# Dividing the attention probabilities by their sums: by a diagonal of reciprocals inside the turning product, in place of a multiplication on GpSimd

## The chip, the core and the metric

The kernel runs on one core of a Trainium2 chip. The metric is the device time of one execution in microseconds (us). A core has five engines that each work through a queue of their own in order: TensorE (PE in the profile, its weight loads PEld), VectorE (DVE), ScalarE (ACT), GpSimd (POOL) and SyncE (SP, which here issues most transfers). They wait for one another by semaphores.

## The reference

One layer: a normalised and modulated input is projected once; half of the width goes through an RWKV-7 recurrence, half through latent attention with 8 heads of 64 (scores over 64 + 32 rotary columns); both halves are gated, projected back and normalised. What the change touches is the attention of 1024 queries over 1024 keys:

```python
def causal_block_attention(q_nope, q_rope, k_nope, k_rope, v):
    scale = (MLA_NOPE + MLA_ROPE) ** -0.5
    ...
    s = (jnp.einsum('bqhd,bkhd->bhqk', qn_b, k_nope)
         + jnp.einsum('bqhd,bkd->bhqk', qr_b, k_rope)).astype(jnp.float32) * scale
    s = jnp.where(key_idx[None, :] <= q_idx[:, None], s, -jnp.inf)
    prob = jax.nn.softmax(s, axis=-1).astype(v.dtype)
    return jnp.einsum('bhqk,bkhd->bqhd', prob, v)
```

So each row of probabilities is the exponential of the scores less their maximum, divided by its own sum.

## The kernel before

Products that need more precision than one pass of TensorE gives are made of three: each operand is split into a high and a low part (type fp32r), and high by high, high by low and low by high are added in PSUM. The program has three long stretches. Up to about 650 us of the span the projections, the recurrence and the preparation of queries, keys and values run interleaved. From 650 to about 822 us the attention runs. From there to the end the output projection (lines 1160 to 1162) and the last normalisation run.

The attention is a loop over 64 steps (`seq`, lines 1196 to 1240): four pairs of heads, in each pair two heads, in each head eight blocks i = 0 to 7 of 128 queries. A step with block i handles (i + 1) blocks of 128 keys, since the rest is masked; a head thus has 1 + 2 + ... + 8 = 36 blocks of 128 x 128, and the stage 288. The parts of a step are:

- `scores` (lines 1059 to 1074): three products per half of the keys into `sp` (PSUM, two buffers), and a small one in bf16 that adds the causal mask.
- `softmax_a` (line 1079): the row maximum `mx` on VectorE, scaled on line 1080.
- `softmax_b`: the exponential on ScalarE from `sp` to `pr` (SBUF, three buffers), which also gives the row sums `sm` (line 1087); the reciprocal on VectorE (line 1088); and the multiplication of `pr` by it on GpSimd, in pieces of up to 512 columns (line 1091).
- `turn_pe` (line 1098): for each block of 128 keys a transpose of `pr` on TensorE into `tp` (PSUM, two buffers of four blocks), so that keys lie on the partitions.
- `turn_evac`: the high part `PTh` on ScalarE (line 1107), the low part `PTl` on VectorE (line 1108).
- `mix` (lines 1119 and 1120): once for two blocks of queries, the values times `PTh` and `PTl` into `op` (PSUM); `gate` (lines 1134 and 1136): two copies on ScalarE (`oc`, `od`), two operations on GpSimd.

In loop step t the program writes the scores and the maximum of step t + 2, the turning of step t, the mixing of steps before, and then the exponential, the reciprocal and the division of step t + 2. So between the end of a division and its turning two steps lie. The queries and keys of the next pair (`heads_qk`, lines 828 to 830, with copies on lines 847 and 848) and the weights for them are spread over the same steps. A scheduler of the framework sets the final order of each engine's queue from this text and its own costs; the loop asks for a priority that keeps near the written order.

Of the kernel before, what the change touches and what calls it, by code (L numbers as in the profile page):

```python
# [17 lines left out]
F32 = mybir.dt.float32  # L18
# [4 lines left out]
ALU = mybir.AluOpType  # L23
# [4 lines left out]
P = 128  # L28
# [3 lines left out]
HALF = 512  # L32
# [54 lines left out]
def hymba_kernel(ctx: ExitStack, tc: tile.TileContext, x, pos, cols, cst, winit, w_ada, b_gate, w_in, w_lora, w0,  # L87
                 w_uqn, w_uqr, w_k, w_v, w_out, final_g, out, dbg=None):
    nc = tc.nc
    V, A, G, T, SY = nc.vector, nc.scalar, nc.gpsimd, nc.tensor, nc.sync  # L90
# [5 lines left out]
    def pool(stack, name, bufs=1, **kw):  # L96
        if kw.get("space") is not DRAM:
            kw["reuse_waits"] = "tile"
        return stack.enter_context(tc.tile_pool(name=name, bufs=bufs, **kw))
# [12 lines left out]
    def cs(name):  # L112
        a, n = _CS[name]
        return cstt[:, a: a + n]

    ident = cs("ident")
# [52 lines left out]
    evp = pool(ctx, "evp")  # L169
# [885 lines left out]
    V.tensor_scalar(rsn[:], rs[0][:], -SCALE, None, ALU.mult)  # L1055

    PTs, probs, tail, ocs, od = {}, {}, [], {}, {}

    def scores(hp, s, i):

# [22 lines left out]
    def softmax_b(i, sp, mx):  # L1083
        n = (i + 1) * P
        pr = at.tile([P, S], F32, tag="pr", name="pr", bufs=3)
        sm = at.tile([P, 1], F32, tag="sm", name="sm", bufs=4)
        A.activation(pr[:, 0:n], sp[:, 0:n], AF.Exp, scale=rss[:, i:i + 1], bias=mx[:], accum_out=sm[:])  # L1087
        V.reciprocal(sm[:], sm[:])  # L1088
        for a in range(0, n, HALF):
            e = min(n, a + HALF)  # L1090
            G.tensor_scalar(pr[:, a:e], pr[:, a:e], sm[:], 1.0, ALU.mult, ALU.mult)  # L1091
        return pr

    def turn_pe(hp, s, i, j0, pr):
        m = min(4, i + 1 - j0)
        tp = psB.tile([P, 4, P], F32, tag="tp", name="tp", bufs=2)
        for j in range(m):
            T.transpose(tp[:, j, :], pr[:, (j0 + j) * P:(j0 + j + 1) * P], ident)  # L1098
        return tp

    def turn_evac(hp, s, i, j0, tp):
# [93 lines left out]
    with tc.high_priority(offset=0):  # L1195
        for t in range(-AHEAD, N + 2):
            sp = mx = op = None
            if 0 <= t + AHEAD < N:
                hp, s, i = seq[t + AHEAD]
# [8 lines left out]
            if sp is not None:  # L1208
                hp, s, i = seq[t + AHEAD]
                mx = softmax_a(i, sp)  # L1210
            if 0 <= t < N:
                hp, s, i = seq[t]
# [6 lines left out]
            if t >= 2 and seq[t - 2][2] % 2 == 1:  # L1219
                hp, s, i = seq[t - 2]  # L1220
                op = mix(hp, s, i // 2)
            if sp is not None:
                probs[t + AHEAD] = softmax_b(seq[t + AHEAD][2], sp, mx)
            if op is not None:
                hp, s, i = seq[t - 2]
# [160 lines left out]
```

## Time and profile before

| | us |
|---|---|
| median of 3 runs | 933.34 |
| the runs | 2558.89, 925.86, 933.34 |
| the profiled execution, its own time | 920.99 |
| its span, first to last instruction | 918.8 |
| granted TensorE clock, mean over the span | 0.973 |

| stretch of the span, us | length | PE | DVE | ACT | POOL busy |
|---|---|---|---|---|---|
| 0 to 650 | 650 | 590.32 | 396.49 | 310.56 | 182.05 |
| 650 to 822 (attention) | 172 | 156.11 | 134.94 | 139.27 | 87.05 |
| 822 to 918.8 | 96.8 | 88.89 | 43.85 | 26.64 | 27.08 |

A line of the profile names the line of the kernel, the engine, the operation, the tile that is written and the ones that are read, and how often it ran. Matmuls follow each other in a pipeline: a record's duration goes on after the next one has started, so what a matmul costs in a row of them is the distance between two starts, not its duration. Of the runs, 2558.89 us is not used.

### The profile page before, as it was taken

How to read it: one execution, taken by the hardware profiler on the slowest of the kernel's cores; microseconds unless marked ns; L12 is line 12 of the kernel's file. 1: busy time of each engine (PE TensorE's matmuls, PEld its weight loads, DVE VectorE, ACT ScalarE, POOL GpSimd, SP SyncE). 2: the span in 40 equal slices, each digit the busy share in tenths (PEclk: the TensorE clock that was granted, in tenths of full speed). 3: DMA queues.
4: the chain of work that ended last, by engine and by line, in shares of the span. 5: the costliest groups of instructions: out<-in, count | busy, mean ns of one | idle time of the engine just before them, and what ended most of it. 6: DMA issues, size and time to landing. Idle time of an engine off the chain costs nothing.

```text
span 918.8 us, 16567 instructions
## 1 busy us (share of the span) xinstructions
PE 835.3 (91%) x5812; PEld 641.2 (70%) x5812; DVE 575.3 (63%) x1462; ACT 476.5 (52%) x1112; POOL 296.2 (32%) x351
## 2 busy tenths in 40 slices
PE   1798997999999999898899999997799998989996
PEld 0586785776777777566667767765678777868885
DVE  5795349378495654955757366247778788765443
ACT  2655332444644636346245464554778888873311
POOL 1311423131232323423133122223436454454400
PEclk9999999999999999998999999999999999999998
DMA  8764433333435324435333254157102031017233
GB/s 253 247 194 153 140 110 115 95 105 88 134 118 150 118 69 135 121 69 165 118 99 104 65 151 139 49 172 203 55 18 70 21 110 59 1 56 239 85 126 126
DMA packets 131714, 106.66 MB, mean 116 GB/s; under 512 B 40616, under 2 KB 108464, under 8 KB 131632
## 3 DMA queue, kind: packets, MB, share of 16 engines
q1 hardware_dynamic: 130672, 102.46, 37.5%
q0 software_dynamic: 960, 3.15, 1.5%
q8 instruction: 46, 0.75, 0.3%
q14 instruction: 36, 0.29, 0.1%
HBM read 76.46 MB, written 29.10 MB: 115 GB/s over the span
## 4 chain that ended last, share of the span: by engine, by line
PE 66%; DVE 13%; ACT 9%; issue 4%; DMA 4%; POOL 2%; SPq 1%; POOLq 0%; DVEq 0%; ACTq 0%
PE mm L164 10%; PE mm L165 8%; PE mm L166 8%; PE po L1160 3%; PE po L1162 3%; PE po L1161 3%; PE gps L577 3%; ACT pr L1087 2%; DVE wtmp L625 2%; DVE W L627 2%; PE tp L1098 2%; ACT PTh L1107 1%; PE rc L712 1%; PE rc L694 1%; PE Y L728 1%
## 5 line engine op out<-in xcount | busy, mean ns | idle before, releaser
L164 PE MATMUL mm<-hTh,whi 128*128 128x512 f32 (+1 forms) x384 | 167.2, 435 | 3.1 <-DVE wtmp L625 2.3
L166 PE MATMUL mm<-hTh,wlo 128*128 128x512 f32 (+1 forms) x384 | 156.9, 409 | 0.0
L165 PE MATMUL mm<-hTl,whi 128*128 128x512 f32 (+1 forms) x384 | 156.8, 408 | 0.0
L157 POOL TENSOR_TENSOR wlo<-wraw,whi 128x512 fp32r<-128x512 f32 (+1 forms) x54 | 71.4, 1323 | 233.8 <-ACT whi L156 215.4
L164 PEld LDWEIGHTS mm<-hTh,whi 128*128 128x128 f32 (+1 forms) x384 | 73.3, 191 | 24.0 <-issue 3.1
L166 PEld LDWEIGHTS mm<-hTh,wlo 128*128 128x128 f32 (+1 forms) x384 | 73.2, 191 | 17.7
L165 PEld LDWEIGHTS mm<-hTl,whi 128*128 128x128 f32 (+1 forms) x384 | 73.5, 191 | 14.6 <-issue 1.4
L1091 POOL TENSOR_SCALAR pr<-pr,sm 128x512 f32<-128x512 f32 (+2 forms) x96 | 55.6, 588 | 72.4 <-DVE sm L1088 50.2
L627 DVE TENSOR_TENSOR W<-W,wtmp 128x60 f32<-128x60 f32 (+24 forms) x248 | 71.5, 288 | 5.8 <-DVE wtmp L625 0.3
L625 DVE TENSOR_TENSOR wtmp<-W,N 128x60 f32<-128x60 f32 (+24 forms) x248 | 69.2, 279 | 5.5
L156 ACT CAST whi<-wraw 128x512 fp32r<-128x512 f32 (+1 forms) x54 | 32.7, 607 | 59.4 <-PE mm L165 36.6
L720 ACT ACTIVATE ST<-rc,eL 64x64 f32<-64x64 f32 x120 | 37.1, 309 | 46.2 <-PE rc L712 44.5
L1087 ACT ACTIVATE pr<-sp,mx,rss 128x128 f32<-128x128 f32 (+3 forms) x64 | 53.3, 834 | 14.8 <-DVE mx L1080 12.3
L1108 DVE TENSOR_TENSOR PTl<-tp,PTh 128x512 fp32r<-128x512 f32 (+2 forms) x96 | 52.2, 553 | 11.8 <-ACT PTh L1107 10.1
L1079 DVE TENSOR_REDUCE mx<-sp 128x1 f32<-128x128 f32 (+3 forms) x64 | 48.0, 750 | 11.4 <-PE sp L1073 11.1
L1160 PE MATMUL po<-wo,yh 128*128 128x512 f32 x128 | 50.3, 393 | 0.8 <-ACT od L1134 0.8
L1107 ACT CAST PTh<-tp 128x512 fp32r<-128x512 f32 (+2 forms) x96 | 44.0, 477 | 13.1 <-PE tp L1098 10.2
L1098 PE MATMUL tp<-cstt,pr 128*128 128x128 f32 x288 | 45.0, 277 | 5.9 <-POOL pr L1091 2.9
L1162 PE MATMUL po<-wo,yl 128*128 128x512 f32 x128 | 50.3, 393 | 0.0
L1161 PE MATMUL po<-wo,yh 128*128 128x512 f32 x128 | 50.3, 393 | 0.0
L1119 PE MATMUL op<-PTh,Vt 128*128 128x256 f32 (+1 forms) x160 | 42.1, 293 | 5.1 <-ACT od L1134 5.1
L584 DVE TENSOR_TENSOR GA<-gps,cstt 128x512 f32<-128x512 f32 x32 | 21.4, 684 | 29.4 <-PE Y L728 22.6
(279 smaller groups left out, 1934.0 us busy)
## 6 DMA issues: line engine op xcount, KB each, us to landing
wraw<-in_w_in SPq DMA_DIRECT2D x52, 256.0 KB, 3.1
wa<-in_w_ada SPq DMA_DIRECT2D x64, 128.0 KB, 3.1
xt<-in_x SPq DMA_DIRECT2D x8, 512.0 KB, 7.4
wg<-in_w_ada SPq DMA_DIRECT2D x32, 128.0 KB, 2.5
N<-d_n SPq DMA_DIRECT2D x32, 128.0 KB, 3.1
wor<-in_w_out SPq DMA_DIRECT2D x16, 256.0 KB, 3.1
cr<-d_c SPq DMA_DIRECT2D x14, 256.0 KB, 3.4
d_c<-craw SPq DMA_DIRECT2D x10, 256.0 KB, 2.2
```

What stands on the lines that cost most here:

```text
L157: G.tensor_tensor(lo[:, :, :m], raw[:, :, :m], hi[:, :, :m].bitcast(F32), ALU.subtract)
L164: T.matmul(ps[:m], lhsT=hi[:, k % 4, :m], rhs=a, start=first, stop=False)
L165: T.matmul(ps[:m], lhsT=hi[:, k % 4, :m], rhs=b, start=False, stop=False)
L166: T.matmul(ps[:m], lhsT=lo[:, k % 4, :m], rhs=a, start=False, stop=last)
L625: V.tensor_tensor(t, W[:, 0:n, u:u + 1].to_broadcast([P, n, m]), N[:, u:u + 1, u + 1:32].to_broadcast([P, n, m]), ALU.mult)
L627: V.tensor_tensor(W[:, 0:n, u + 1:32], W[:, 0:n, u + 1:32], t, ALU.subtract)
L1087: A.activation(pr[:, 0:n], sp[:, 0:n], AF.Exp, scale=rss[:, i:i + 1], bias=mx[:], accum_out=sm[:])
L1091: G.tensor_scalar(pr[:, a:e], pr[:, a:e], sm[:], 1.0, ALU.mult, ALU.mult)
L1098: T.transpose(tp[:, j, :], pr[:, (j0 + j) * P:(j0 + j + 1) * P], ident)
L1160: T.matmul(ps, lhsT=yh[k][:, ts_], rhs=hi, start=first, stop=False)
L1161: T.matmul(ps, lhsT=yh[k][:, ts_], rhs=lo, start=False, stop=False)
L1162: T.matmul(ps, lhsT=yl[k][:, ts_], rhs=hi, start=False, stop=last)
```

## The change

The multiplication of the whole of `pr` by the reciprocals goes. In its place GpSimd multiplies the 128 x 128 identity by the reciprocals of the step's 128 rows, which gives a diagonal matrix `dg`, one of four in a new tile `dgs`. The turning is no longer a transpose with the identity but a plain FP32 product of the block of `pr` (stationary) with `dg` (moving): a transpose whose columns are divided by the sums. `dgs` takes one of the two buffers of the tag `p2`, which is shared with the normalisation of the recurrence (`post`) and with the squares of the last stage (line 1286 before).

```diff
@@ -1055,6 +1055,7 @@
     PTs, probs, tail, ocs, od = {}, {}, [], {}, {}
+    dgs = evp.tile([P, 4, P], F32, tag="p2", name="dgs", bufs=2)
 
@@ -1086,16 +1087,17 @@
         V.reciprocal(sm[:], sm[:])
-        for a in range(0, n, HALF):
-            e = min(n, a + HALF)
-            G.tensor_scalar(pr[:, a:e], pr[:, a:e], sm[:], 1.0, ALU.mult, ALU.mult)
-        return pr
-
-    def turn_pe(hp, s, i, j0, pr):
+
+        dg = dgs[:, i % 4]
+        G.tensor_scalar(dg, ident, sm[:], 1.0, ALU.mult, ALU.mult)
+        return pr, dg
+
+    def turn_pe(hp, s, i, j0, prob):
+        pr, dg = prob
         m = min(4, i + 1 - j0)
         tp = psB.tile([P, 4, P], F32, tag="tp", name="tp", bufs=2)
         for j in range(m):
-            T.transpose(tp[:, j, :], pr[:, (j0 + j) * P:(j0 + j + 1) * P], ident)
+            T.matmul(tp[:, j, :], lhsT=pr[:, (j0 + j) * P:(j0 + j + 1) * P], rhs=dg, start=True, stop=True)
         return tp
```

The scheduler also orders the queues a little differently in the attention; outside it the order stays. Lines behind line 1058 move down by one, behind line 1091 by two. Three places show it.

GpSimd, in the third pair of heads (`wor` and `gb` belong to the output projection, `yg` and `oc` to `gate`). Before:

```order
L1153 TENSOR_TENSOR wor<-wor,gb 128x512
L1091 TENSOR_SCALAR pr<-pr,sm 128x256
L1136 TENSOR_TENSOR oc<-oc,od 128x256
L1136 TENSOR_TENSOR yg_7452<-oc,yg_7452 128x256
L1091 TENSOR_SCALAR pr<-pr,sm 128x384
L1091 TENSOR_SCALAR pr<-pr,sm 128x512
```

With the change:

```order
L1155 TENSOR_TENSOR wor<-wor,gb 128x512
L1092 TENSOR_SCALAR dgs<-cstt,sm 128x128 x2
L1138 TENSOR_TENSOR oc<-oc,od 128x256
L1138 TENSOR_TENSOR yg_7445<-oc,yg_7445 128x256
L1092 TENSOR_SCALAR dgs<-cstt,sm 128x128 x2
```

One or two multiplications for a step, of up to 512 columns each, have become one of 128 columns for each of the 64 steps, and the diagonal of one step more stands ahead of the two operations of `gate`.

TensorE, in the second pair of heads, the turning of the step with block i = 5 (six blocks of keys) amid the mixing of the steps before. Before:

```order
L1119 MATMUL op<-PTh,Vt 128x256
L1120 MATMUL op<-PTl,Vt 128x256
L1098 MATMUL tp<-cstt,pr 128x128 x4
L1119 MATMUL op<-PTh,Vt 128x128
L1120 MATMUL op<-PTl,Vt 128x128
L1098 MATMUL tp<-cstt,pr 128x128 x2
L1069 MATMUL sp<-kt_6872,qt_6873 128x128
```

With the change:

```order
L1121 MATMUL op<-PTh,Vt 128x256
L1122 MATMUL op<-PTl,Vt 128x256
L1121 MATMUL op<-PTh,Vt 128x128
L1100 MATMUL tp<-dgs,pr 128x128 x6
L1122 MATMUL op<-PTl,Vt 128x128
L1070 MATMUL sp<-kt_6872,qt_6873 128x128
```

The six turnings now stand together, behind the last but one product of the mixing and ahead of the next scores.

ScalarE, a little further in the same pair. Before:

```order
L1087 ACTIVATE pr,sm<-sp,mx,rss 128x896
L1107 CAST PTh<-tp 128x4x128
L1134 COPY oc<-op 64x256
L1107 CAST PTh<-tp 128x2x128
L1134 COPY od<-op 64x256
L1087 ACTIVATE pr,sm<-sp,mx,rss 128x1024
```

With the change:

```order
L1088 ACTIVATE pr,sm<-sp,mx,rss 128x896
L1109 CAST PTh<-tp 128x4x128
L1109 CAST PTh<-tp 128x2x128
L1088 ACTIVATE pr,sm<-sp,mx,rss 128x1024
L1136 COPY oc<-op 64x256
L1136 COPY od<-op 64x256
```

The exponential of the widest block now stands ahead of the two copies that free `op`.

## The prediction

> **What bounds the kernel now.** I read the page from the top, then the busy time in the three stretches of the span, then the attention alone: its groups, its waits, and its instructions in order of time.
>
> ```profile
> span 918.8 us, 16567 instructions
> ```
>
> ```profile
> core 0: us, PE busy (x) PEld busy (x) DVE busy (x) ACT busy (x) POOL busy (x), PEclk, DMA share, GB/s
> 0.00:650.00 650.00, 590.32 (x4389) 437.58 (x4389) 396.49 (x1068) 310.56 (x724) 182.05 (x181) 0.97 0.45 131
> 650.00:822.00 172.00, 156.11 (x1039) 131.61 (x1039) 134.94 (x329) 139.27 (x330) 87.05 (x145) 1.00 0.15 46
> ```
>
> The change touches only the stretch from 650 to 822 us, the attention. There TensorE shows 156.11 us of 172 at full granted clock, so 15.9 us of open idle time; ScalarE 139.27, VectorE 134.94, GpSimd 87.05. What the change takes from, GpSimd, is the emptiest of the four, and what it adds to, TensorE, the fullest. What is removed and what waits on it, from the groups and the waits of that stretch:
>
> ```profile
> L1091 POOL TENSOR_SCALAR pr<-pr,sm 128x512 f32<-128x512 f32 (+2 forms) x96 | 55.6, 588 | 72.4 <-DVE sm L1088 50.2 <-DVE mx L1080 9.2 <-PE qkps L830 5.8
> ```
>
> ```profile
> PEld tp L1098 <- POOL pr L1091: 6.0, 10, 1.4
> ...
> PE tp L1098 <- POOL pr L1091: 2.9, 4, 1.1
> ```
>
> GpSimd multiplies for 55.6 us but stands idle 72.4 us before it, waiting for the sums: it follows the softmax, it does not hold it up much. TensorE waits for its result 14 times, 6.0 us seen from the weight loads and 2.9 from the matmuls. So the division is mostly latency that two steps of lead cover.
>
> How full TensorE really is, the busy time does not tell, because a record goes on after the next has started. The distances do:
>
> ```profile
> 699.61 0.39 PE L1069 MATMUL sp<-kt,qt 96*128 96x512 f32 x1
> 699.84 0.39 PE L1070 MATMUL sp<-kt,qt 96*128 96x512 f32 x1
> ...
> 700.29 0.28 PE L1069 MATMUL sp<-kt,qt 96*128 96x256 f32 x1
> 700.40 0.28 PE L1070 MATMUL sp<-kt,qt 96*128 96x256 f32 x1
> ...
> 701.39 0.22 PE L1119 MATMUL op<-PTh,Vt 128*128 128x128 f32 x1
> 701.45 0.27 PE L1120 MATMUL op<-PTl,Vt 128*128 128x128 f32 x1
> ...
> 702.91 0.34 PE L1070 MATMUL sp<-kt,qt 96*128 96x384 f32 x1
> 703.08 0.34 PE L1071 MATMUL sp<-kt,qt 96*128 96x384 f32 x1
> ```
>
> A matmul of 512 columns is followed after 0.23 us, of 384 after 0.17, of 256 after 0.11 to 0.12, of 128 after 0.06. The counts in the stretch, of which lines 1070, 1071 and 829, 830 repeat those of 1069 and 828, and 1120 that of 1119:
>
> ```profile
> L1098 PE MATMUL tp<-cstt,pr 128*128 128x128 f32 x288 | 45.0, 277 | 5.9 <-POOL pr L1091 2.9 <-DVE PTl L1108 2.6
> L1119 PE MATMUL op<-PTh,Vt 128*128 128x256 f32 x128 | 36.0, 309 | 5.1 <-ACT od L1134 5.1
> ...
> L1069 PE MATMUL sp<-kt,qt 96*128 96x512 f32 x48 | 20.8, 432 | 2.9 <-ACT pr L1087 2.9
> ...
> L828 PE MATMUL qkps<-cqh,wqh 128*128 128x512 f32 x18 | 8.3, 463 | 1.8 <-DVE mx L1080 1.2 <-DVE kt L848 0.6
> ...
> L1069 PE MATMUL sp<-kt,qt 96*128 96x384 f32 x16 | 5.9, 370 | 0.2 <-ACT pr L1087 0.2
> ...
> L828 PE MATMUL qkps<-ckvh,wkh 128*128 128x512 f32 x11 | 5.0, 459 | 0.0
> ...
> L1069 PE MATMUL sp<-kt,qt 96*128 96x256 f32 x15 | 4.4, 292 | 0.0
> ```
>
> Of 512 columns 3 x (48 + 18 + 11) = 231, 53 us; of 384, 3 x 16 = 48, 8 us; of 256, 2 x 128 + 3 x 15 = 301, 35 us; of 128 without the turning some 170, 11 us; the 288 transposes at 0.11 us, 31 us. Together 138 of 172 us: TensorE is the fullest engine, with 34 us in which nothing starts, of which 15.9 are open idle.
>
> **The change part by part.** *The turning.* It is the only price. A transpose and a plain FP32 product of the same size stand both in the trace of before, at full clock: line 536 (transposes) and line 524 (FP32 products, 128 x 128 by 128 x 128), each four per unit and eight units, so 32 in the program.
>
> ```profile
> L524 PE MATMUL cps<-cstt,z 128*128 128x128 f32 x64 | 9.7, 294 | 0.0
> ...
> L536 PE MATMUL kps<-cstt,sq 128*128 128x128 f32 x32 | 5.1, 281 | 0.0
> ```
>
> ```profile
> 91.66 1.05 PE L524 MATMUL cps<-cstt,z 128*128 128x128 f32 x8
> ...
> 108.31 0.60 PE L536 MATMUL kps<-cstt,sq 128*128 128x128 f32 x4
> ```
>
> 32 transposes are 32 records, 32 products are 64: a plain FP32 product is issued twice. The distances are alike: (0.60 - 0.28) / 3 = 0.11 us between transposes, (1.05 - 0.28) / 7 = 0.11 us between the records of line 524 (0.28 is the duration of the last one, from the means of 281 and 294 ns). So a turning goes from 0.11 to 0.22 us, and 288 of them add 288 x 0.11 = 32 to 33 us of TensorE's time; I take 33. The weight loads double in number too and lie beside the matmuls, as they do in line 524, whose distance holds them. The Trainium skill's page "Perfetto Trace Analysis", section "Transposes", speaks against this edit as well: a logical transpose should be issued as one and not as a standard matmul, because special logic then skips the arithmetic. It gives no price; these two rows do.
>
> *How much of the 33 us shows.* TensorE's starts would fill 138 + 33 = 171 of 172 us. The bounds are -1 us (every gap of the 34 us takes up added work) and +33 us (none does). Between them I go by the second pair of heads, cut where blocks i = 0 to 2, 3 to 5 and 6 to 7 of each of its two heads are turned:
>
> ```profile
> 694.66:700.71 6.05, 6.05 (x42) 5.25 (x42) 4.34 (x13) 4.90 (x14) 4.48 (x7) 1.00 0.01 4
> 700.71:710.75 10.04, 9.38 (x58) 7.52 (x58) 9.35 (x22) 9.66 (x21) 4.25 (x8) 1.00 0.39 131
> 710.75:715.80 5.05, 4.75 (x37) 4.10 (x36) 3.08 (x10) 3.54 (x11) 2.64 (x6) 1.00 0.11 29
> 715.80:723.90 8.10, 7.81 (x51) 6.64 (x51) 5.78 (x14) 5.34 (x14) 1.57 (x3) 1.00 0.00 0
> 723.90:733.45 9.55, 8.59 (x57) 7.14 (x56) 8.28 (x18) 9.12 (x21) 5.79 (x10) 1.00 0.11 28
> 733.45:737.82 4.37, 4.37 (x37) 3.79 (x35) 3.81 (x12) 3.42 (x9) 3.15 (x6) 1.00 0.64 184
> ```
>
> Columns are PE, PEld, DVE, ACT, POOL. Blocks 0 to 2 hold 6 turnings (0.7 us more), 3 to 5 hold 15, 6 and 7 again 15 (1.7 us more each). In the second and fifth row ScalarE works 9.66 of 10.04 and 9.12 of 9.55 us: ScalarE sets those, and I cost the 1.7 us there at nothing; if that cover were gone, they would cost 3.4 us a pair, 14 over four. In the other four rows TensorE is all but closed, and the rise less the open idle is 0.7 + (1.7 - 0.3) + (0.7 - 0.3) + 1.7 = 4.2 us; over four pairs 17 us. Closed by records is not closed by starts: half of the 34 us does not show as open idle, and taking from each row the gaps between starts (0.6, 0.9, 0.9 and 0.5 us in those four) leaves about 2 us a pair, 8 over four. I take 12 us, midway, because some of these gaps are waits that move along with TensorE.
>
> *The division.* 96 multiplications, 55.6 us, go; 64 of 128 columns come. The same size stands in the row of durations:
>
> ```profile
> L1091 POOL TENSOR_SCALAR pr<-pr,sm x96: 367/637/727, 650.4 to 816.1; 128x512 f32<-128x512 f32 x48, 128x128 f32<-128x128 f32 x16, 128x256 f32<-128x256 f32 x16, 128x384 f32<-128x384 f32 x16
> ```
>
> 64 x 0.37 = 24 us, so GpSimd loses 32 us that lie beside TensorE's work. Between the reciprocal and the turning there is 0.37 us instead of 0.37 for one block and up to 2 x 0.69 for eight. This is never longer than before, and it takes from the 8.9 us of waits above; they are part of the gaps that I let the rise fill, so they are not counted again. The two operations of `gate` on GpSimd come earlier. A diagonal waits for the turning of the step four before, since there are four, and the turning is two steps behind: no wait. The buffer of `p2` is used before by the recurrence's normalisation, which ends ahead of the attention, and next by the squares of the last stage, whose inputs come after the last turning: nothing.
>
> *The order.*
>
> ```profile
> 732.55 1.21 ACT L1087 ACTIVATE pr<-sp,mx,rss 128x1024 f32<-128x1024 f32 x1 [0.20 <-POOL pr L1091]
> ```
>
> ScalarE puts this widest exponential ahead of the two copies that free `op`, so the next mixing waits up to 1.2 us longer, eight times at most; TensorE's queue has the turning of seven blocks and the scores of the next step ahead of that mixing, 14 x 0.11 + 0.4 = 2 us. I cost it at nothing, for that reason; without it, up to 10 us.
>
> **The sum.** The profiled execution took 920.99 us by its own time, 2.2 more than its span. 921 + 12 = 933 in its terms. The runs shown are 925.86 and 933.34 (the third, 2558.89, is no measure of the kernel), so 5 and 12 us above the profiled one, and the median is the upper of the two. I add 5: 938 us.
>
> **The rivals.** *The full price.* The rise moves every later instruction: the next scores wait in the same queue behind the turning, the maximum, the exponential and the sums follow from them, and no gap is filled. For it speaks that in two of six rows TensorE has no open idle at all, against it that ScalarE sets two others. It decides once ScalarE waits for the turning longer than now (10.2 us in the stretch):
>
> ```profile
> ACT PTh L1107 <- PE tp L1098: 10.2, 19, 1.5
> ```
>
> 921 + 33 + 5 = 959 us. Chance 0.12.
>
> *The gaps take it all.* On the other side, not slower: the waits of TensorE before the turning end because the diagonal is there 1 us earlier in the wide blocks, the queue closes up, and the stretch stays at 171 to 172 us. For it speak 34 us of gaps for 33 us of work; against it that the gaps do not lie where the wide turnings do: the last of the six rows has 1.7 us more work and the least idle. It decides if the wait for GpSimd vanishes and blocks 6 and 7 take no longer than 4.4 to 5.1 us. 921 + 0 + 5 = 926 us, down to 921. Chance 0.22.
>
> *A product at four transposes.* The mechanism would be that line 524 is cheap for a reason that the new product lacks, and that each turning takes four distances of 0.11 us: 288 x 0.33 = 94 us more, starts for 138 + 94 = 232 us in a stretch of 172, 921 + 60 + 5 = 986 us. The rows of line 524 speak against it; operands of the same type and size take two. Chance 0.02.
>
> The Trainium skill, "TensorE: Matmul & The Clock Gate", section "Terms", says that the transpose mode of this chip is four times faster for FP32, which would be this case; by that rule the sum would be the 986 us above. The trace shows a factor of two.
>
> *One issue per turning.* The product might be issued once, so that the change does not cost what it says; then only GpSimd's latency goes, at most the 8.9 us of waits: 921 - 9 + 5 = 917 us. The 64 records of line 524 speak against it. Chance 0.04.
>
> **How the numbers follow.** The partial price has the remaining 0.60, with a range of its own of 928 to 948 us (2 to 22 us more). The whole range, 923 to 954 us, reaches down into the case where the gaps take all and up into the lower part of the full price, and leaves out the four transposes and the one issue. A difference of over 2% (18.6 us) is about what a measurement of this kernel can tell from none. Slower by that: the full price 0.12, four transposes 0.02, and the top of the partial price 0.06, 0.20. Faster by that: only if one issue and a shorter latency come together, 0.03. Within it 0.77.
>
> **What would show it.** In the profile of the changed kernel: line 1100 with 576 records of matmul, 0.11 us apart; line 1092 with 64 of about 0.37 us, GpSimd's total down by some 30 us; TensorE's busy time in the attention up from 156 to about 170 us, its waits for GpSimd nearly gone; the attention 184 us long instead of 172, the longer steps those of blocks 6 and 7, the steps of blocks 3 to 5 as long as before; everything outside it unchanged. It would be wrong if line 1100 had 288 records or another distance, if the steps of blocks 3 to 5 grew as much as the others (then ScalarE did not cover them), or if the time moved outside the attention.

## The result and the profile after

| | before, us | after, us |
|---|---|---|
| median of four runs each (before: 932.48 without its run of 2558.89) | 932.91 | 952.43 |
| lowest to highest (2558.89 left out) | 925.86 to 933.34 | 947.58 to 958.17 |
| profiled execution, its own time | 920.99 | 958.17 |
| its span | 918.8 | 956.4 |

The changed kernel is slower: 952.43 us. The recorded ratio to before is 1.0272, with a 95% interval of 1.0219 to 1.0325; the medians of the table alone give 1.021. The forecast was 938 us, so the direction was right and the size was not: 20 us between the medians where the forecast lay 5 above the median then known. The time lies in the upper end of the stated range of 923 to 954 us, and among the outcomes slower by over 2%, to which the prediction gave 0.20. Both profiled executions stand at the edge, before's below all its timed runs and after's the slowest of its own, so the two profiles lie 37 us apart and not 20. Where that comes from is seen when both spans are cut in three: ahead of the first exponential, the attention, and from the first product of the output projection on. Columns are length, then PE, PEld, DVE, ACT and POOL busy, the granted clock, the DMA share and GB/s. Before, in these exact cuts:

```profile
0.00:649.60 649.60, 589.95 (x4389) 437.58 (x4389) 396.13 (x1067) 310.16 (x723) 182.05 (x181) 0.97 0.45 131
649.60:823.00 173.40, 156.63 (x1042) 131.66 (x1040) 135.31 (x330) 140.47 (x333) 87.07 (x146) 1.00 0.15 45
823.00:918.80 95.80, 88.74 (x384) 72.00 (x384) 43.85 (x66) 25.83 (x58) 27.06 (x25) 0.98 0.42 143
```

After:

```profile
0.00:658.60 658.60, 601.04 (x4387) 445.92 (x4388) 396.45 (x1066) 310.43 (x722) 183.07 (x181) 0.95 0.45 129
658.60:860.60 202.00, 192.75 (x1332) 170.76 (x1331) 136.75 (x330) 140.67 (x333) 55.50 (x114) 0.98 0.12 39
860.60:956.40 95.80, 88.73 (x384) 71.99 (x384) 44.42 (x66) 25.53 (x58) 27.01 (x25) 0.98 0.42 143
```

The last stretch has not changed at all. The first one is 9 us longer with the same instructions, at a granted clock of 0.95 instead of 0.97. That belongs to this execution and not to the change: in a second profile of the changed kernel it is 655.0 us long, and in a kernel without the change ("No division at all" below) 659.7. The attention is 28.6 us longer. There TensorE's busy time went up by 36 us, GpSimd's went down by 32, and VectorE's and ScalarE's stayed within 1.5 us. Its granted clock is 0.98. In the profiles of this case the clock is either full or half (a stretch at 0.50 is shown with the single issues below), so that is 0.02 x 2 x 202 = 8 us at half, and by estimate up to 4 us lost.

What the changed lines do, from the groups of the attention after:

```profile
L1100 PE MATMUL tp<-dgs,pr 128*128 128x128 f32 x576 | 81.7, 285 | 6.8 <-DVE PTl L1110 6.1 <-DVE sm L1089 0.4
L1100 PEld LDWEIGHTS tp<-dgs,pr 128*128 128x128 f32 x576 | 72.1, 195 | 11.3 <-issue 7.4 <-DVE PTl L1110 1.8 <-POOL dgs L1092 0.7
...
L1092 POOL TENSOR_SCALAR dgs<-cstt,sm 128x128 f32<-128x128 f32 x64 | 24.1, 376 | 131.3 <-DVE sm L1089 84.5 <-DVE mx L1081 25.9 <-PE sp L1074 11.7
```

And the instructions of TensorE in order of time, in the second pair of heads after:

```profile
744.76 1.11 PE L1100 MATMUL tp<-dgs,pr 128*128 128x128 f32 x8
745.63 0.36 PE L1121 MATMUL op<-PTh,Vt 128*128 128x256 f32 x1
...
752.28 1.58 PE L1100 MATMUL tp<-dgs,pr 128*128 128x128 f32 x12 [0.48 <-DVE PTl L1110]
...
754.90 1.80 PE L1100 MATMUL tp<-dgs,pr 128*128 128x128 f32 x14 [0.29 <-DVE PTl L1110]
```

288 turnings are 576 records, and 8 of them take 745.63 - 744.76 = 0.87 us, 0.11 us each. The diagonals are 64 of 376 ns. TensorE's waits for GpSimd, 6.0 and 2.9 us before, are 0.7 us. The price of the turning is thus as forecast: 288 x 0.11, about 33 us of starts. What was not as forecast is how much of it shows. Counted as in the prediction, with the distances of each width, TensorE's starts fill 172 of the 202 us after and 138 of 173 before; 30 us are left without a start, where there were 35. Only some 5 of the 33 us went into the gaps.

Where the gaps went on is seen on the other engines. Before, ScalarE waited 10.2 us for the turning; the other two of its chain of softmax were:

```profile
ACT pr L1087 <- DVE mx L1080: 12.3, 19, 1.5
...
DVE sm L1088 <- ACT pr L1087: 7.8, 13, 0.8
```

After:

```profile
ACT PTh L1109 <- PE tp L1100: 29.8, 37, 1.5
...
ACT pr L1088 <- DVE mx L1081: 23.0, 26, 2.1
DVE sm L1089 <- ACT pr L1088: 18.6, 35, 0.8
```

ScalarE now waits for the turning 37 times instead of 19, and the maximum and the sums come later with it: VectorE and ScalarE moved along with TensorE's queue. The stretch of the second pair of heads that the prediction cut in six rows, cut again at the same turnings:

```profile
710.52:716.77 6.25, 6.25 (x46) 5.60 (x45) 3.98 (x11) 3.61 (x10) 3.10 (x6) 1.00 0.01 3
716.77:727.71 10.94, 10.82 (x72) 9.33 (x70) 8.51 (x17) 8.61 (x21) 1.72 (x4) 1.00 0.35 107
727.71:734.78 7.07, 6.70 (x49) 6.09 (x49) 4.64 (x16) 4.82 (x12) 1.86 (x5) 1.00 0.12 39
734.78:743.44 8.66, 8.59 (x59) 7.51 (x60) 5.56 (x14) 5.28 (x14) 0.75 (x2) 1.00 0.01 2
743.44:753.58 10.14, 9.66 (x66) 8.46 (x65) 7.46 (x16) 7.29 (x18) 2.80 (x5) 1.00 0.08 27
753.58:761.34 7.76, 7.27 (x60) 6.59 (x58) 4.79 (x16) 5.98 (x15) 4.72 (x8) 1.00 0.42 137
```

They are longer by 0.20, 0.90, 2.02, 0.56, 0.59 and 3.39 us, 7.7 in all. The rows of blocks 3 to 5, the second and the fifth, grew by 0.9 and 0.6 us though ScalarE, which filled them before with 9.66 and 9.12 us, has only 8.61 and 7.29 us in them now: part of its work has moved into neighbouring rows (the third has 1.3 us more of it, the sixth 2.6), and TensorE is the fullest engine of these rows now. The rows of blocks 6 and 7, the third and the sixth, grew by 5.4 us.

### The profile page after: what moved, and what is told of

Read it like the earlier page. It is cut to its first block, busy times and chain, and to the rows that moved or that the text cites. A ratio compares the mean times of both kernels' runs of the same rounds, so it can differ in the third digit from the quotient of the medians.

```text
span 956.4 us, 17083 instructions
## 1 busy us (share of the span) xinstructions
PE 882.5 (92%) x6100; PEld 688.7 (72%) x6100; DVE 577.6 (60%) x1462; ACT 476.6 (50%) x1112; POOL 265.6 (28%) x319
## 4 chain that ended last, share of the span: by engine, by line
PE 66%; DVE 16%; ACT 8%; DMA 4%; issue 4%; POOL 1%; SPq 1%; DVEq 0%; POOLq 0%; ACTq 0%
PE mm L164 8%; PE mm L165 7%; PE mm L166 7%; PE tp L1100 5%; PE po L1162 3%; PE po L1163 3%; PE po L1164 3%; DVE W L627 3%; DVE wtmp L625 3%; PE gps L577 3%; ACT pr L1088 2%; PE Y L728 1%; PE rc L694 1%; PE Y L725 1%; PE rc L712 1%
## 5 line engine op out<-in xcount | busy, mean ns | idle before, releaser
L1100 PE MATMUL tp<-dgs,pr 128*128 128x128 f32 x576 | 81.7, 285 | 6.8 <-DVE PTl L1110 6.1
L166 PEld LDWEIGHTS mm<-hTh,wlo 128*128 128x128 f32 (+1 forms) x384 | 74.4, 194 | 18.1
L1100 PEld LDWEIGHTS tp<-dgs,pr 128*128 128x128 f32 x576 | 72.1, 195 | 11.3 <-issue 7.4
L625 DVE TENSOR_TENSOR wtmp<-W,N 128x60 f32<-128x60 f32 (+24 forms) x248 | 71.5, 288 | 5.5
L627 DVE TENSOR_TENSOR W<-W,wtmp 128x60 f32<-128x60 f32 (+24 forms) x248 | 68.8, 278 | 5.8 <-DVE wtmp L625 0.3
L1092 POOL TENSOR_SCALAR dgs<-cstt,sm 128x128 f32<-128x128 f32 x64 | 24.1, 376 | 131.3 <-DVE sm L1089 84.5
L1109 ACT CAST PTh<-tp 128x512 fp32r<-128x512 f32 (+2 forms) x96 | 43.6, 479 | 31.1 <-PE tp L1100 29.8
```

The lines of the kernel that those rows point to most:

```text
L166: T.matmul(ps[:m], lhsT=lo[:, k % 4, :m], rhs=a, start=False, stop=last)
L625: V.tensor_tensor(t, W[:, 0:n, u:u + 1].to_broadcast([P, n, m]), N[:, u:u + 1, u + 1:32].to_broadcast([P, n, m]), ALU.mult)
L627: V.tensor_tensor(W[:, 0:n, u + 1:32], W[:, 0:n, u + 1:32], t, ALU.subtract)
L1100: T.matmul(tp[:, j, :], lhsT=pr[:, (j0 + j) * P:(j0 + j + 1) * P], rhs=dg, start=True, stop=True)
```

## The experiments

The theory after the result: the price is the time in which TensorE issues the second half of each turning, and the 34 us without a start are no free room, because most of them are latencies between the engines that move along when TensorE's queue grows. The rivals: that something particular to the FP32 product or to the diagonal costs the time; that the other order of the queues does; that the buffers of `tp`, which VectorE frees late, make the gaps; and that TensorE was not the bound before, so that its added work shows from some point on only. Each time below is a median with the lowest and highest run in brackets, and each ratio, with its 95% interval, stands against the kernel before on the same chip. The median of before was 934.68 us beside the first four kernels (the changed kernel once more, transposes twice, the product, no division), 929.60 beside the next four (the two kernels with part of the turnings, the single issue, the late division), 926.13 beside the two pairs after them (the order, the buffers) and 929.36 beside the last three.

**The changed kernel once more.**

> The changed kernel once more, beside the others. First theory (TensorE's queue is the path through the attention, so the second issue of each turning costs nearly its whole 33 us there): attention about 200 us long instead of 173, matmul starts fill about 172 of them, time 950 +- 5 us. Second theory (the long attention of the first profile came from its clock drop and from waits that vary): attention 185 to 190 us.

952.76 us (948.4 to 957.45), ratio 1.0187 (1.0101 to 1.0272), with an attention of 201.0 us: the length of the first theory.

**The price without the product.** The kernel before, each transpose issued twice; the division stays on GpSimd.

```diff
-            T.transpose(tp[:, j, :], pr[:, (j0 + j) * P:(j0 + j + 1) * P], ident)
+            for _ in range(2):
+                T.transpose(tp[:, j, :], pr[:, (j0 + j) * P:(j0 + j + 1) * P], ident)
```

> The kernel before, with each transpose of the turning issued twice into the same place (the second overwrites the first with the same values); the division stays on GpSimd. First theory (issue time in TensorE's queue is what costs): 288 more issues at 0.109 us, 31 us, of which all but some 5 us show: 25 us more than before, about 955 us. Second theory (the plain FP32 product has a price of its own, by its longer weight loads of 0.19 us, that a repeated transpose does not have): 940 us or less. Third theory (the gaps of the attention take added work up): 935 us.

951.51 us (947.75 to 955.39), ratio 1.0173 (1.0086 to 1.026). Its attention, with GpSimd still at 87 us:

```profile
650.60:850.70 200.10, 187.22 (x1331) 163.91 (x1330) 136.87 (x330) 140.68 (x332) 87.35 (x145) 0.99 0.12 39
```

That is the time and the stage of the changed kernel with neither a product nor a diagonal in it. What costs is the second issue, whatever it is. It costs 17 us and not the 25 that were expected: of 32 us of added starts about half shows.

**The product without the diagonal.** A plain FP32 product with the identity, the division on GpSimd as before.

```diff
-            T.transpose(tp[:, j, :], pr[:, (j0 + j) * P:(j0 + j + 1) * P], ident)
+            T.matmul(tp[:, j, :], lhsT=pr[:, (j0 + j) * P:(j0 + j + 1) * P], rhs=ident, start=True, stop=True)
```

> The product alone: the turning is a plain FP32 product with the identity, the division stays on GpSimd over the whole of pr as before. First theory: 20 to 30 us more than before, and within 5 us of the changed kernel, since GpSimd's latency lies in gaps that the longer turning closes: 950 to 960 us. Second theory (the diagonal gave back the 9 us of waits for GpSimd, and the product cost so much more): 960 us or more. Third theory (the diagonal itself brought the new waits): 938 us, as forecast for the product.

956.33 us (951.61 to 959.51), ratio 1.0236 (1.014 to 1.0332). The turning has the row of the changed kernel:

```profile
L1098 PE MATMUL tp<-cstt,pr 128*128 128x128 f32 x576 | 81.5, 285 | 7.7 <-DVE PTl L1108 7.1
```

The difference to the changed kernel beside it is 3.6 us, the worth of taking the division off GpSimd once the turning is dear, and the intervals overlap. So do those of this kernel and of the transposes issued twice, 4.8 us apart: no price of the product beyond its second issue is shown.

**No division at all.** The kernel before without the division of `pr`; this leaves the division out.

```diff
-        for a in range(0, n, HALF):
-            e = min(n, a + HALF)
-            G.tensor_scalar(pr[:, a:e], pr[:, a:e], sm[:], 1.0, ALU.mult, ALU.mult)
         return pr
```

> The division left out (the probabilities stay undivided, nothing else divides them); the turning stays a transpose. It shows the most that taking the division off GpSimd can give. First theory: the waits of TensorE for it, 6.0 and 2.9 us, go in part: 3 to 8 us less than before, 923 to 928 us. Second theory (two steps of lead cover the division): no difference, 930 us. Third theory (GpSimd's latency sets many of the 34 us of gaps): 15 us less or more, 915 us.

925.93 us (917.11 to 930.86), ratio 0.9889 (0.9793 to 0.9985): 9 us less than before, by the interval anything from 1 to 19. That is about what the change could have won on GpSimd's side. In its profile the attention is 171.1 us long at a clock of 0.99, 2 us less than before. The 55.6 us of multiplications are thus worth about a sixth of their length, which fits their lying beside TensorE's work.

**Part of the turnings.** The diagonal for blocks 3 to 5 alone, and for blocks 6 and 7 alone (`(6, 7)` in the condition), 120 of the 288 turnings in each; the rest as before. Against the changed kernel, in part:

```diff
+        if i in (3, 4, 5):
+            dg = dgs[:, i % 4]
+            G.tensor_scalar(dg, ident, sm[:], 1.0, ALU.mult, ALU.mult)
+            return pr, dg
...
+            if dg is None:
+                T.transpose(tp[:, j, :], pr[:, (j0 + j) * P:(j0 + j + 1) * P], ident)
```

> The diagonal and the plain product only in the steps of blocks 3, 4 and 5 (15 of a head's 36 turnings); the other steps divide on GpSimd and turn by transpose as before. The forecast held that these steps are ScalarE's and that the second issue costs nothing there. First theory now (the second issue costs nearly everywhere alike): 15/36 of the 18 to 20 us, 8 us more than before, about 940 us, with the attention some 10 us longer. The forecast's: 0 to 2 us more, 933 us.

> The same in the steps of blocks 6 and 7 alone (the other 15 of a head's 36 turnings). First theory: 8 us more than before, 940 us, no more than with blocks 3 to 5. The forecast's: two to three times the price of blocks 3 to 5, 10 us more, since TensorE is closed there and not there.

Blocks 3 to 5: 935.04 us (928.36 to 947.07), ratio 1.0055 (1.0012 to 1.0098), 5.4 us. Blocks 6 and 7: 939.24 us (934.54 to 941.98), ratio 1.0106 (1.0075 to 1.0136), 9.6 us. The same 14 us of added starts cost more where TensorE is closed than where ScalarE was full, as the prediction had it, but they are not free in either: both intervals lie above 1. They overlap, so the order of the two is likely and not sure.

**One issue instead of two.** The changed kernel with `pr` and `dgs` in fp32r, which makes each turning a single issue; this gives up precision in the probabilities.

```diff
-    dgs = evp.tile([P, 4, P], F32, tag="p2", name="dgs", bufs=2)
+    dgs = evp.tile([P, 4, P], F32R, tag="p2", name="dgs", bufs=2)
...
-        pr = at.tile([P, S], F32, tag="pr", name="pr", bufs=3)
+        pr = at.tile([P, S], F32R, tag="pr", name="pr", bufs=3)
```

> The changed kernel with the probabilities and the diagonal in the type fp32r, so that the product of a turning is issued once; this gives up precision of the probabilities (they are rounded to fp32r before the turning). First theory (the number and length of issues is the whole price): at the 0.06 us between matmuls of 128 columns the turning takes 17 us instead of 65, and the division's waits are gone as well: attention 160 us or less, 8 to 15 us less than the kernel before, 918 to 925 us. Second theory (the diagonal's own chain or the scheduler's order is the price): no less than before, 932 us or more.

961.63 us (953.29 to 967.32), ratio 1.032 (1.0225 to 1.0414), slower than before and than the changed kernel. The expectation took 0.06 us for a turning. The trace has more:

```profile
725.76 0.64 PE L1100 MATMUL tp<-dgs,pr 128*128 128x128 f32 x4
726.24 0.33 PE L1121 MATMUL op<-PTh,Vt 128*128 128x256 f32 x1
...
726.53 0.23 PE L1121 MATMUL op<-PTh,Vt 128*128 128x128 f32 x1
726.59 0.28 PE L1122 MATMUL op<-PTl,Vt 128*128 128x128 f32 x1
726.70 0.45 PE L1070 MATMUL sp<-kt,qt 96*128 96x512 f32 x1
```

Four turnings take 0.48 us, 0.12 us each, about what four transposes take. The 0.06 us stands between the two products of 128 columns at 726.53 and 726.59; behind the second of them it is 0.11. So TensorE has half the records of the changed kernel for the turning, but no fewer starts to fill than the kernel before, about 138 us. The order of its queue is that of the changed kernel. What differs is the clock, the column behind POOL. The attention in pieces, then a stretch of it that lies wholly at half clock, with four of its turnings:

```profile
662.60:700.00 37.40, 35.84 (x168) 30.62 (x168) 23.72 (x61) 23.38 (x59) 8.17 (x21) 0.71 0.09 22
700.00:750.00 50.00, 44.74 (x274) 39.09 (x274) 35.05 (x88) 36.42 (x87) 14.74 (x31) 0.93 0.12 39
750.00:800.00 50.00, 43.38 (x242) 37.62 (x241) 34.08 (x81) 35.60 (x82) 14.59 (x26) 0.83 0.24 74
800.00:866.50 66.50, 59.97 (x364) 53.33 (x362) 42.75 (x102) 47.02 (x107) 18.12 (x35) 0.87 0.06 21
...
662.60:677.60 15.00, 15.00 (x50) 12.34 (x50) 9.04 (x26) 9.11 (x24) 4.66 (x12) 0.50 0.10 27
...
672.99 1.09 PE L1100 MATMUL tp<-dgs,pr 128*128 128x128 f32 x4
673.89 0.52 PE L1121 MATMUL op<-PTh,Vt 128*128 128x256 f32 x1
```

The clock is 0.71 to 0.93, where before had 1.00 and after 0.98, and at half clock a turning takes 0.90 / 4 = 0.22 us. 0.29 x 2 x 37.4 + 0.07 x 2 x 50 + 0.17 x 2 x 50 + 0.13 x 2 x 66.5 = 63 us were at half, which by estimate costs up to 31 us of the 204. That would leave 173 us at full clock, the length before: without the second issue, the diagonal, the shorter work on GpSimd and the new order of TensorE's queue would together neither cost nor win anything. It is an estimate, since the fall of the clock is not explained. What fewer starts are worth this kernel cannot say, since it has none fewer than before; the last three do.

**A division behind the mixing.** The reciprocals go to DRAM and come back as rows laid over the partitions, and GpSimd multiplies the rows of `oc` (64 of each head) by them; the turnings are transposes again. The main lines:

```diff
+            SY.dma_start(d_rs[hp, hd][0, gs].rearrange("(b p) -> p b", p=P), rv[:])
+            if hd:
+                for h2 in range(2):
+                    SY.dma_start(rbs[h2 * 64:h2 * 64 + 64, i // 2 % 2], d_rs[hp, h2][:, gs].to_broadcast([64, 256]))
...
+                    G.tensor_tensor(oc, oc, rbs[:, g % 2], ALU.mult),
```

> The division moved out of the turning and off the probabilities: they stay undivided, turned by transpose as before; the reciprocals of two blocks of queries go to DRAM and come back as rows laid over 64 partitions, and GpSimd multiplies the head's output (128 x 256, once for two blocks and two heads) by them in the gate. TensorE gets nothing to do. If the waits for the division are worth what the run without a division showed (8.8 us less at the medians), this takes most of it: 4 to 9 us less than before, 925 to 930 us. Against it: 96 more transfers on SyncE's queue, whose waits may hold up the weights behind them: then no difference, or more than before.

1118.18 us (1116.99 to 1129.81), ratio 1.2052 (1.1965 to 1.214). Expected were 925 to 930 us, or more if the queue held things up. The idea was lost to its transport, as the waits of SP's queue and of VectorE show (us in total, times, the longest):

```profile
SPq L1099 <- DMA d_rs<-rv: 292.1, 32, 11.6
...
DVE rv L1093 <- DMA d_rs<-rv: 109.9, 19, 9.4
```

SP's queue stood 32 times, 9 us on the mean, until a store of the reciprocals had landed, before it could issue the load that reads them back; VectorE waited for the same stores before it could write the next reciprocals. It says nothing on the division itself. (The kernel adds 32 stores and 32 loads, not the 96 transfers of the expectation.)

**The order.** Both kernels with TensorE's queue held to the order in which the program is written, the same in both.

```diff
-    with tc.high_priority(offset=0):
+    with tc.high_priority(offset=0), tc.manual_schedule(engines={mybir.EngineType.PE}):
```

> The kernel before with TensorE's queue held to the written order of the attention loop (the other engines are left to the scheduler). It is one half of a pair with the next kernel, in which TensorE's queue has the same instructions in the same places. By itself it may be some us slower than before: 930 to 945 us.

> The changed kernel with TensorE's queue held to the same written order. First theory (the second issue of each turning is paid wherever TensorE is the engine waited for; the order has little part in it): 16 to 26 us more than its partner. Second theory (half of the loss came from the scheduler's new order, which stands the turnings of neighbouring steps close together): 10 us more than its partner or less.

Before: 962.81 us (953.91 to 970.38), ratio 1.0367 (1.0281 to 1.0453). With the change: 985.99 us (981.65 to 991.09), 1.0651 (1.058 to 1.0722). The written order is worse for both, more than was expected, with twice the gaps, and the change costs 23.2 us in it. So the order that the scheduler gave TensorE's queue in the changed kernel is not the cause. The other engines' queues were left to the scheduler in both, and were not tested.

**The buffers of `tp`.** VectorE computes the low part from the high part alone, so that `tp` is free when ScalarE has read it; the low part becomes zero, which leaves it out.

```diff
-        V.tensor_tensor(tl[:, 0:m, bs], tp[:, 0:m], th[:, 0:m, bs].bitcast(F32), ALU.subtract)
+        V.tensor_tensor(tl[:, 0:m, bs], th[:, 0:m, bs].bitcast(F32), th[:, 0:m, bs].bitcast(F32), ALU.subtract)
```

> The changed kernel, in which VectorE computes the low part from the high part alone instead of from tp (so the low part of the probabilities is zero: left out), with as many instructions as before; tp is free as soon as ScalarE has copied it. In the changed kernel the gaps ahead of turnings are 16 of 30 us. First theory (two buffers of tp hold the turnings up: a turning waits until VectorE has done with the tile two before): these gaps halve and the time falls by 8 us or more, to 943 us. Second theory (the gaps come from the chain of scores, maximum, exponential, sums): 3 us or less, 949 us.

> The same edit in the kernel before (low part of the probabilities left out, tp free after ScalarE's copy). There few gaps wait for tp (2.6 us by the waits). First theory: 0 to 4 us less than before, so less than the edit gives the changed kernel. If it gives as much as there, the edit speeds up VectorE's chain in general and says nothing of tp.

In the changed kernel: 954.45 us (947.46 to 962.62), ratio 1.0283 (1.0194 to 1.0373), no gain on 952.4. In the kernel before: 939.95 us (937.34 to 946.08), ratio 1.0172 (1.0093 to 1.0251), a loss of 14 us where 0 to 4 less were expected. TensorE's wait for the low part, 6.1 us ahead of the turnings, is gone in the changed kernel; waits for ScalarE's copy (3.5 us) and for the diagonal (1.9 us) stand in its place, and the gaps ahead of the turnings are about 15 us, where there were 16. So the release of `tp` by VectorE does not hold them by itself. The edit does more than release `tp`: with both operands read from SBUF, VectorE's operation takes longer, and so do GpSimd's multiplications beside it. Before, and with the edit:

```profile
L1108 DVE TENSOR_TENSOR PTl<-tp,PTh 128x512 fp32r<-128x512 f32 (+2 forms) x96 | 52.2, 553 | 11.8 <-ACT PTh L1107 10.1 <-PE op L1120 0.4
L1108 DVE TENSOR_TENSOR PTl<-PTh 128x512 fp32r<-128x512 f32 (+2 forms) x96 | 61.7, 654 | 11.5 <-ACT PTh L1107 10.4
...
L1091 POOL TENSOR_SCALAR pr<-pr,sm 128x512 f32<-128x512 f32 x48 | 33.2, 695 | 50.9 <-DVE sm L1088 36.2 <-PE qkps L830 5.8 <-PE sp L1073 4.1
L1091 POOL TENSOR_SCALAR pr<-pr,sm 128x512 f32<-128x512 f32 x48 | 40.4, 845 | 42.2 <-DVE sm L1088 29.4 <-DVE mx L1080 7.5 <-PE tp L1098 2.6
```

In the changed kernel VectorE's operation went from 553 to 600 ns. Whether the 14 us come from these longer operations or from the other order of the queues that the scheduler chose was not tested, and a small gain in the changed kernel may hide behind them.

**How much of an added start shows.** The last question was whether the kernel before stands on a slope or at a knee. Three kernels: before and after without the values' product with the low part of the probabilities (this leaves that part out; VectorE and ScalarE still compute it), and before with each transpose issued three times.

```diff
-            T.matmul(op[:, a:256], lhsT=lw, rhs=th[:, j % 4, a:256], start=j == 0, stop=False)
-            T.matmul(op[:, a:256], lhsT=lw, rhs=tl[:, j % 4, a:256], start=False, stop=j == nj - 1)
+            T.matmul(op[:, a:256], lhsT=lw, rhs=th[:, j % 4, a:256], start=j == 0, stop=j == nj - 1)
```

> The kernel before without the values' product with the low part of the probabilities (line 1120): 160 matmuls, about 16.7 us of TensorE's starts, go; the low part itself is still computed, so VectorE and ScalarE do the same as before. This leaves out the low part. TensorE's starts in the attention fall from 138 to about 121 us. Theory A, the stage is TensorE's starts plus about 30 us of waits that move along, at any amount of work: the stage goes from 173 to about 155 us and the time to 912 to 918 us, ratio 0.98. Theory B, the kernel before stands at a knee, below which the softmax on VectorE, ScalarE and the latency between them set the stage: stage 168 to 173 us, time 925 to 932 us, ratio 0.99 to 1.00, gaps up to 45 to 50 us. Theory C, less work on TensorE brings a lower granted clock, as in the kernel with single issues: tens of us at half clock, ratio above 1.01.

> The changed kernel without the values' product with the low part of the probabilities (this leaves out the low part): starts fall from 172 to about 155 us. Theories A and B alike: stage 184 to 188 us, 13 to 17 us less than the changed kernel's 201; time 935 to 940 us, ratio to before 1.005 to 1.012, as when the diagonal was used for half of the turnings. If the changed kernel's gaps came from somewhere other than the amount of TensorE's work (the order, the diagonal's latency), the stage would stay above 195 us and the ratio at 1.02.

> The kernel before with each transpose issued three times, division on GpSimd as before: 864 records, starts 138 + 64 = 202 us in the attention. Theories A and B: the gaps stay near 30 us, stage about 232 us, time 980 to 986 us, ratio 1.05 to 1.055; each third issue costs the whole 32 us that it adds. If the gaps can take work, less: ratio under 1.04.

Before, short: 919.18 us (911.86 to 925.75), ratio 0.9887 (0.9846 to 0.9928). After, short: 936.15 us (933.83 to 940.52), 1.0113 (1.0051 to 1.0175). Three issues: 976.31 us (973.28 to 980.82), 1.0534 (1.0476 to 1.0593). Their attentions, before short:

```profile
662.30:827.60 165.30, 146.11 (x883) 116.72 (x882) 132.87 (x331) 138.71 (x332) 86.80 (x145) 0.97 0.15 47
```

Three issues:

```profile
651.00:877.90 226.90, 216.49 (x1619) 196.48 (x1618) 140.21 (x330) 142.06 (x333) 87.41 (x145) 0.98 0.11 35
```

The kernels with the scheduler's order and a clock of 0.97 or more, by TensorE's starts in the attention (counted from the distances):

| kernel | starts, us | stage, us | without a start, us | time less that of before, us |
|---|---|---|---|---|
| before, short | 122 | 165.3 | 43 | -10.2 |
| no division | 138 | 171.1 | 33 | -8.8 |
| before | 138 | 173.4 | 35 | 0 |
| before, early release of `tp` | 138 | 184.2 | 46 | +13.8 |
| diagonal in blocks 3 to 5 | 152 | 181.9 | 30 | +5.4 |
| diagonal in blocks 6 and 7 | 152 | 184.7 | 33 | +9.6 |
| after, short | 153 | 181.3 | 28 | +6.8 |
| transposes twice | 170 | 200.1 | 30 | +16.8 |
| after, beside it | 172 | 201.0 | 29 | +18.1 |
| after, early release of `tp` | 172 | 200.1 | 28 | +28.3 |
| product, division on GpSimd | 172 | 203.4 | 31 | +21.6 |
| transposes three times | 201 | 226.9 | 26 | +47.0 |

The last column is the difference of the medians on one chip; the others come from one profile of each kernel. That of before, short, took 925.66 us, 6 more than its median, and was at half clock for 9 us of the attention, so that some 4 of its 43 us belong to the clock.

With the division on GpSimd throughout, the time grows by 10.2 us for 16 us of starts (from 122 to 138), by 16.8 for the next 32 (to 170) and by 30.2 for the next 31 (to 201): 0.6, 0.5 and nearly all of it. With the diagonal, 5.4 to 9.6 us for 14 (138 to 152) and about 11 for 19 (153 to 172), 0.4 to 0.7. So the kernel before stands on a slope, and no knee shows up to 172; above it the slope is steeper. These are rough figures. The medians of before run from 926.13 to 934.68 us between the chips: the changed kernel with the early release stands 10 us above its fellow in the last column, though its own time is only 2 us longer. And an edit moves more than starts: the same 138 us of them stand at -8.8, 0 and +13.8 us.

The first of the last three kernels, 919.18 us, lies between the two theories, just above the 912 to 918 of starts plus a constant; the second came out in time as both had it (its stage, 181.3 us, is shorter than their 184 to 188); the third is 4 us below what both had. So the stage is not quite starts plus a constant, and it is not held by the softmax either: the time without a start shrinks slowly, from 43 to 26 us, as TensorE fills, and even with 63 us more to do than before it leaves 26. Less work did not cost clock here (0.97).

## Why the prediction was wrong

- **The fullest engine.** Right. What was added to TensorE showed in part, and all that was taken from GpSimd was worth about 9 us. (Of the 72.4 us of GpSimd's idle time that the prediction put down to the sums, its row gives them 50.2.)
- **The turning, 0.11 to 0.22 us, 33 us in all.** Right: 576 records 0.11 us apart. The 0.06 us for 128 columns is true of some products only (0.06 and 0.11 in the rows of the single issue); the sum of 138 us shifts by a few us with it, alike in all kernels. The Trainium skill's page "TensorE: Matmul & The Clock Gate", section "Terms", by which the transpose would have been four times cheaper, does not hold for these operands: two issues of 0.11 us against one, here and in the kernel with plain products. The Trainium skill's page "Perfetto Trace Analysis", section "Transposes", advises against a standard matmul in place of a transpose; these runs agree and put the price to it: 21.6 us for 288 of them in the kernel with plain products.
- **"How much of the 33 us shows", 12 us.** This is the step that failed. Measured are 20 us between the medians, 18 when both ran on one chip again, and 23 in the pair with a fixed order of TensorE's queue. What it put at nothing was blocks 3 to 5: "ScalarE sets those, and I cost the 1.7 us there at nothing". Alone they cost 5.4 us (1 to 9 by the interval). ScalarE's 9.66 of 10.04 us said that the row was full, not that its work had to stay in that row: the loop runs two steps ahead, and in the changed kernel part of ScalarE's work lies in neighbouring rows. Cutting a pipelined stage into rows and giving each to its fullest engine counted as cover what was only the present phase of the two queues. Blocks 6 and 7 came out as sized when they alone were changed: by the prediction's rows their share was 2.0 to 3.1 us a pair, 8 to 12 over four, and they cost 9.6. In the changed kernel their rows grew by more, 5.4 us in the pair that was cut, with the work of ScalarE that had moved into them; the 15 us of the two kernels together make up most of the 18 to 20, and the steps of blocks 0 to 2 were not tried alone.
- **The gaps as room.** The lower end of that step let the gaps between starts take up whatever lay beside them. With 14 us more they stood at 30 to 33 us, with 33 us more at 30. Some of them close, and most move along. The prediction's own signal for this came true: it said the full price decides once ScalarE waits for the turning longer than 10.2 us, and ScalarE waits 29.8. The full price itself, 33 us, was not reached either; about 0.6 of it shows.
- **The division, nothing of its own.** Nearly right. Leaving it out is worth about 9 us while the turning is cheap; taking it off GpSimd is worth 3.6 us, within the error, when the turning is dear.
- **The order, nothing.** Right as far as the pair with a fixed order tells: about the same price with identical queues on TensorE. ScalarE's order, the widest exponential ahead of the two copies, was not held, and its "up to 10 us" was not tested.
- **Outside the attention.** Right: the last stretch is 95.8 us in both. The 9 us ahead of the attention are the clock of the profiled execution.
- **The 5 us to the median.** Mis-sized too, and it makes up half of the miss. The median of before stands 12 us above its profiled execution (932.91 against 920.99), as the median then shown did; the prediction added the distance of the faster run. So 921 + 12 + 5 = 938 is in the same terms 921 + 20 + 12 = 953: of some 14 us missed, 7 to 8 are the price and 7 the base. The profile of before had a full clock in the attention (1.00), which no profile of the other kernels repeated (at best 0.99), so its 921 us were a low base, and the difference between the two profiles is too high a price.
- **The signs.** The records, their distance and the diagonals came as foretold. TensorE's busy time was foretold at about 170 us and is 192.75, the attention at 184 and is 202 (201 in the second profile). The steps of blocks 3 to 5 did not stay as long as before, but grew less than those of 6 and 7, so the sign named for this error was not clear in the profile; the kernel with these blocks alone showed it.

Why the stage gives about 0.6 and not 0 or 1 for each added microsecond is argued and not shown: the waits of ScalarE for the turning, of the exponentials for the maximum and of the sums for the exponentials grow together (10.2, 12.3 and 7.8 us before, 29.8, 23.0 and 18.6 after), which fits a ring of latencies through TensorE, ScalarE and VectorE, and no single wait was found whose removal closes the gaps.

## What to carry to other kernels

Time on the fullest engine in which nothing starts is not room for more work: add to it, and price the addition at half to all of its issue time, as it was in this kernel, unless a run shows that the gap closes. Take the distance from a row of the very instruction: 128 columns were 0.06 us in one place and 0.11 to 0.12 in another. Moving work from an emptier engine to the fullest one can win at most what leaving that work out wins, which a single run tells (here 9 us), while its price on the full engine (here 33 us of issue time) can be read from two rows of the trace. A row that another engine fills is no cover where the program runs steps ahead, because that engine's work can move to the next row.

## What the runs showed of the hardware

- The FP32 product of 128 x 128 by 128 x 128 is two records 0.11 us apart, a transpose of the same size is one record, and so is a product in fp32r: 576, 288 and 288 for the same turnings. The single product in fp32r is followed after 0.12 us, no sooner than a transpose.
- In the kernel with single issues in fp32r the granted clock of the attention was 0.85 on the mean, and both kernels with TensorE's queue in written order had 0.94 and 0.95, against 0.97 to 1.00 in the others, leaving aside the one whose queues stood still for the stores. Less work on TensorE alone (122 us of starts) kept 0.97, and the kernel before, with as many starts as the one with single issues, had 1.00. What took the clock down is open.
- VectorE's subtraction of up to 128 x 512 took longer on the mean with both operands read from SBUF than with one of them read from PSUM (654 and 600 ns against 553), and GpSimd's multiplication of 128 x 512 beside it 845 ns instead of 695.
- A store of 256 reciprocals of 4 bytes each, spread over DRAM by partition, kept the waiting queue for about 9 us each time (292.1 us in 32 waits).
